# A hybrid decoder block on one core: the two-level FFN products with the weight sums of the second product traced one tile later, the fourth token-side sum traced inside the first tile, and the first tile's operands in other buffers

## The chip, the cores and the metric

The kernel is one program on one core of a Trainium2 chip. The metric is the device time of one execution in microseconds (us); smaller is better. The engines are PE (TensorE), DVE (VectorE), ACT (ScalarE), POOL (GpSimd) and SP (SyncE, which here only issues DMAs). Times inside the program count from the first instruction of the profiled execution (the span's start).

## The reference, cut to what matters

One layer of a hybrid block over 1024 tokens and 16 meta tokens, model width 1024: three mixers (window attention, forgetting attention, a gated recurrence), merged and added to the residual, and then the FFN, which is where the change lies:

```
u = rms_norm(h, norm_ffn[l])
gate_ff, up_ff = jnp.split(u @ w_ffn_in[l], 2, axis=-1)
h = h + (jax.nn.silu(gate_ff) * up_ff) @ w_ffn_out[l]
...
return rms_norm(h, norm_final)[:, N_META:]
```

`w_ffn_in` is 1024 x 5632 (2816 gate columns and 2816 up columns), `w_ffn_out` is 2816 x 1024.

## The kernel before

**Precision.** Every matrix operand is split into a high part (an ACT copy, line 118) and a low part (a DVE subtraction of the high part from the value, line 119); a product is three matmuls (high x high, high x low, low x high, line 150). So each operand costs one ACT and one DVE instruction before PE may use it.

**The FFN's first product.** The 2816 features are 22 tiles of 128. Feature tiles `j` (0 to 10) and `j + 11` form a pair. The tokens are two halves of 512, kept as feature-major operands `u2[0]` and `u2[1]`, each in quarters (`b11`, `b21` of the first half of the tokens, `b12`, `b22` of the second). Pair 0 is computed plainly by `swiglu_plain(0)` and `swiglu_plain(11)`. All other tiles use a two-by-two Strassen-like scheme in `swiglu(f, ...)`: seven `product` calls of 12 matmuls each instead of eight. Its token-side operands are `b11`, `b21`, `b22` and four sums `t1` to `t4`, which `combine()` makes once for all tiles: DVE subtractions and additions on 128x1024 pieces (in rotating buffers `fo`, four of them), and then a split of each. Its weight-side operands are `a11`, `a12` (halves of the gate weights), `a21`, `a22` (halves of the up weights) and sums of these that POOL makes (`a21 - a11`, `s2 = a22 - a21`, `a11 + s2`, `a12 - s2`). `operand` splits a weight-side half into one buffer: the tag `wh` (two buffers), `wl` (two) or `ar` (three).

The seven products of one `swiglu`, in PE's order, by the names of the profile: `a11*b11` into `mm_s` (operand in `wh`), `a12*b21` into `sc_s` (in `wl`), `s2*t2` on top of `mm_s` (in `ar`), `(a11+s2)*t1` into `tr_s` (in `ar`), `a21*t3` on top of `mm_s` (in `ar`), `(a12-s2)*b22` on top of `tr_s` (in `wh`), and `a22*t4` on top of `mm_s` (in `wl`). Before the third product may add to `mm_s`, ACT copies it out (line 952); that copy is named `c`. Results go to the tag `a` (six buffers, two for each `swiglu`).

**Sums for the FFN's second product.** The second product, `product2` at the end, is a two-by-two scheme of the same kind over all 11 pairs. Its sums are made pair by pair in the loop over `j`: `combine_w(j)` loads two tiles of `w_ffn_out` into `fo` buffers, makes four POOL sums and writes four pieces to DRAM (`bsp`); `combine_a(j, a11, a21, a12, a22)` takes the pair's four results, makes four POOL sums and writes six pieces (`asp`); `spill(0, j, ...)` writes the seventh.

**What sets the order.** The Tile framework places every instruction in its engine's queue at compile time. The place in the program is a priority: of the instructions that its planner holds to be ready, the earliest in the program goes first, so a later instruction can stand ahead of an earlier one that isn't ready. Buffers of a tag are handed on when all readers of the old content are done. At run time each queue is in order.

Of the kernel before, what the change touches and what calls it, by code (L numbers as in the profile page):

```python
# [51 lines left out]
def hybrid_block(ctx, tc, h_in, w_in, w_v0, w_v1, w_bd, par, rows, gains, relt, onehot,  # L52
# [4 lines left out]
    def dma(dst, src):  # L57
        nc.sync.dma_start(f32(dst) if dst.dtype == F32R else dst, f32(src) if src.dtype == F32R else src)
# [8 lines left out]
    wp = ctx.enter_context(tc.tile_pool(name="wstream", bufs=2, side="left"))  # L67
# [11 lines left out]
    def nm(s):  # L79
        uid[0] += 1  # L80
        return f"{s}_{uid[0]}"
# [61 lines left out]
    def mm3(ps, terms, first=True):  # L143

        n = 3 * len(terms)
        cost = ps.shape[-1] / 2.4 + 3
        i = 0
        for ah, al, bh, bl in terms:
            for a, b in ((ah, bh), (ah, bl), (al, bh)):
                pe.matmul(ps, a, b, start=first and i == 0, stop=i == n - 1, skip_group_check=not first)  # L150
                i += 1
            yield 3 * cost

    def run(gen):
        for _ in gen:
            pass
# [38 lines left out]
    def halves(x):  # L195
        return x[:, :512], x[:, 512:]
# [80 lines left out]
    with tc.tile_pool(name="r0", bufs=1, side="right", reuse_waits="tile") as r0:  # L277
# [68 lines left out]
        bb = r0.tile([P, 8, 383], F32, name="bb")  # L346
# [128 lines left out]
    with ExitStack() as ctx2:  # L475
# [247 lines left out]
        ready = set()  # L723
# [32 lines left out]
    mp = ctx4.enter_context(tc.tile_pool(name="m4", bufs=16, side="left", reuse_waits="tile"))  # L756
# [7 lines left out]
    def pair_tile(pl, **kw):  # L764

        return [pl.tile([P, D], F32R, tag="m4", name=nm("pt"), **kw).rearrange("p (k t) -> p k t", k=2)
                for a in range(2)]
# [63 lines left out]
    with tc.tile_pool(name="r4", bufs=1, side="right", reuse_waits="tile") as r4:  # L831
        woh = r4.tile([P, KT, D], F32R, name="woh")
        wol = r4.tile([P, KT, D], F32R, name="wol")
        with tc.tile_pool(name="r4a", bufs=1, side="right", reuse_waits="tile") as r4a:
# [8 lines left out]
            for m in range(8):  # L843
                f, raw = ahead
# [50 lines left out]
    NJ = NF // 2  # L895
# [3 lines left out]
    def sub(eng, o, a, b):  # L899
        eng.tensor_tensor(o, a, b, ALU.subtract)  # L900

    def add(eng, o, a, b):
        eng.tensor_tensor(o, a, b, ALU.add)

    with tc.tile_pool(name="r5", bufs=1, side="right", reuse_waits="tile") as r5:
        def t5(tag, bufs, n=512):
            return r5.tile([P, n], F32, tag=tag, bufs=bufs, name=nm(tag))

        def product(ps, a, b, first=True):

            run(mm3(ps, [(a[:, 0, k * P:(k + 1) * P], a[:, 1, k * P:(k + 1) * P],
                          b[k // 2][0][:, k % 2], b[k // 2][1][:, k % 2]) for k in range(4)], first))

        def operand(pl, tag, bufs, src):
            t = pl.tile([P, 2, 512], F32R, tag=tag, bufs=bufs, name=nm(tag))
            split(t[:, 0], t[:, 1], src)
            return t

        def swiglu_plain(f):
            w = [load_w(w_fi[f + NF * i], D) for i in range(2)]  # L920
            at_ = []
            for c in range(2):
                pg, pv = (mm_bank(f"_{x}{f}") for x in "gu")
                for ps, (wh, wl) in zip((pg, pv), w):
                    run(mm3(ps, [(wh[:, k * P:(k + 1) * P], wl[:, k * P:(k + 1) * P],
                                  u2[c][k // 2][0][:, k % 2], u2[c][k // 2][1][:, k % 2]) for k in range(KT)]))
                sg = t5("a", 6)
                act.activation(sg, pg, AF.Sigmoid)
                dve.tensor_tensor(sg, pg, sg, ALU.mult)
                dve.tensor_tensor(sg, pv, sg, ALU.mult)  # L930
                at_.append(sg)
            return at_

        def fetch_fi(f, i):
            w = []
            for s in range(2):
                pl = r5 if i % 2 else wp
                raw = pl.tile([P, D], F32, tag="wr", bufs=2, name=nm("wr"))
                dma(raw, w_fi[f + NF * s])
                w.append(halves(raw))  # L940
            return w

        def swiglu(f, w, bb):

            (a11, a12), (a21, a22) = w
            b11, b21, b22, t1, t2, t3, t4 = bb
            p1, p2, p5 = mm_bank(f"_s{f}"), sc_bank(f"_s{f}"), tr_bank(f"_s{f}")
            g0, g1, u1 = (t5("c", 6) for _ in range(3))
            s0, s1 = (t5("a", 6) for _ in range(2))
            s2 = t5("s2", 2)  # L950
            product(p1, operand(wp, "wh", 2, a11), b11)
            act.activation(g0, p1, AF.Copy)  # L952
            product(p2, operand(wp, "wl", 2, a12), b21)
            add(dve, g0, p2, g0)
            act.activation(s0, g0, AF.Sigmoid)
            dve.tensor_tensor(s0, g0, s0, ALU.mult)
            sub(pool, a21, a11, a21)
            sub(pool, s2, a22, a21)
            product(p1, operand(r5, "ar", 3, s2), t2, False)
            act.activation(g1, p1, AF.Copy)  # L960
            add(pool, a11, s2, a11)
            product(p5, operand(r5, "ar", 3, a11), t1)
            act.activation(u1, p5, AF.Copy)
            product(p1, operand(r5, "ar", 3, a21), t3, False)
            add(dve, u1, p1, u1)
            sub(pool, a12, a12, s2)
            product(p5, operand(wp, "wh", 2, a12), b22, False)
            add(dve, g1, p5, g1)
            act.activation(s1, g1, AF.Sigmoid)
            dve.tensor_tensor(s1, g1, s1, ALU.mult)  # L970
            dve.tensor_tensor(s1, u1, s1, ALU.mult)
            product(p1, operand(wp, "wl", 2, a22), t4, False)
            dve.tensor_tensor(s0, p1, s0, ALU.mult)
            return [s0, s1]

        def combine():

            b11, b21 = u2[0][:2], u2[0][2:]
            b12, b22 = u2[1][:2], u2[1][2:]
            t3 = [pair_tile(r5, bufs=4) for _ in range(2)]  # L980
            t2, t1 = ([pair_tile(mp) for _ in range(2)] for _ in range(2))
            temp = lambda: t5("fo", 4, D).rearrange("p (k t) -> p k t", k=2)
            v2 = []
            for i in range(2):
                v3 = temp()
                v2.append(temp())
                for v, x, y in zip((v3, v2[i]), b22[i], b12[i]):
                    sub(dve, v, f32(x), f32(y))
                add(dve, v3, v3, v2[i])
                for x, y in zip((v3, v2[i]), b11[i]):  # L990
                    add(dve, v2[i], x, f32(y))
                split(*t2[i], v2[i])
                split(*t3[i], v3)
            t4 = [pair_tile(mp) for _ in range(2)]
            for t, b in ((t1, b22), (t4, b21)):
                for i in range(2):
                    v = temp()
                    sub(dve, v, f32(b[i][0]), v2[i])
                    add(dve, v, v, f32(b[i][1]))
                    split(*t[i], v)  # L1000
            return b11, b21, b22, t1, t2, t3, t4

        def spill(i, j, x):
            dma(asp[i][j], x)

        def combine_w(j):

            raws = []
            for i in range(2):
                raw = t5("fo", 4, D)  # L1010
                dma(raw, w_fo[(j + NJ * i) * P:(j + NJ * i + 1) * P])
                raws += halves(raw)
            b11, b12, b21, b22 = raws
            t2 = zp.tile([P, 512], F32, tag="z", bufs=2, name=nm("t2"))
            sub(pool, b12, b22, b12)
            add(pool, t2, b12, b11)
            sub(pool, b11, b22, t2)
            sub(pool, b21, b21, t2)
            for i, x in ((2, t2), (3, b11), (4, b12), (6, b21)):
                dma(bsp[i][j], x)  # L1020

        def combine_a(j, a11, a21, a12, a22):

            s2 = zp.tile([P, 512], F32, tag="z", bufs=2, name=nm("t2"))
            spill(1, j, a12)
            spill(6, j, a22)
            sub(pool, a21, a11, a21)
            sub(pool, s2, a22, a21)
            add(pool, a11, s2, a11)
            sub(pool, a12, a12, s2)  # L1030
            for i, x in ((2, s2), (3, a11), (4, a21), (5, a12)):
                spill(i, j, x)


        for j in range(NJ):
            if j == 0:
                first, second = swiglu_plain(0), swiglu_plain(NJ)
                bb = combine()
                spill(0, j, first[0])
            else:  # L1040
                first = swiglu(j, fetch_fi(j, 0), bb)
                spill(0, j, first[0])
                second = swiglu(j + NJ, fetch_fi(j + NJ, 1), bb)
            combine_w(j)
            combine_a(j, *first, *second)
    ctx4.close()


# [173 lines left out]
```

## Time and profile before

| | us |
|---|---|
| median of 3 runs (1662.05 to 1663.47) | 1662.32 |
| profiled execution, its own time | 1662.29 |
| its span, first to last instruction | 1660.5 |
| PE busy | 1630.2 (98%) |
| DVE busy | 999.4 (60%) |
| ACT busy | 760.7 (46%) |
| POOL busy | 433.1 (26%) |

The span is cut by the work of PE almost everywhere; what lies around the span is 1.8 us. The FFN's plain pair runs from 1008 to 1053 us of the span, the ten pairs of the scheme from there to 1444, and the second product to 1654.

### The profile page before, as it was taken

How to read it: one execution, taken by the hardware profiler on the slowest of the kernel's cores; microseconds unless marked ns; L12 is line 12 of the kernel's file. 1: busy time of each engine (PE TensorE's matmuls, PEld its weight loads, DVE VectorE, ACT ScalarE, POOL GpSimd, SP SyncE). 2: the span in 40 equal slices, each digit the busy share in tenths (PEclk: the TensorE clock that was granted, in tenths of full speed). 3: DMA queues.
4: the chain of work that ended last, by engine and by line, in shares of the span. 5: the costliest groups of instructions: out<-in, count | busy, mean ns of one | idle time of the engine just before them, and what ended most of it. 6: DMA issues, size and time to landing. Idle time of an engine off the chain costs nothing.

```text
span 1660.5 us, 22597 instructions
## 1 busy us (share of the span) xinstructions
PE 1630.2 (98%) x8159; PEld 1375.1 (83%) x8159; DVE 999.4 (60%) x1799; ACT 760.7 (46%) x1397; POOL 433.1 (26%) x341
## 2 busy tenths in 40 slices
PE   7999999999999999999999999899999999999998
PEld 6898978888888888888887888688888888888886
DVE  6565556555566666641348437977666676567544
ACT  6456466555555555542336434333333333345342
POOL 2111001001122221110225001776666566300000
PEclk9999999999999999999999999899999999999999
DMA  7132352223324142339737221464444443598642
GB/s 255 63 108 93 122 153 79 88 89 121 108 76 129 59 122 79 107 114 320 244 127 235 102 77 70 158 222 169 165 147 146 146 161 131 197 356 278 195 128 101
DMA packets 110879, 242.47 MB, mean 146 GB/s; under 512 B 11944, under 2 KB 23544, under 8 KB 110512
## 3 DMA queue, kind: packets, MB, share of 16 engines
q1 hardware_dynamic: 110768, 241.04, 42.7%
q8 instruction: 64, 1.05, 0.3%
q14 instruction: 47, 0.39, 0.1%
HBM read 163.45 MB, written 72.21 MB: 142 GB/s over the span
## 4 chain that ended last, share of the span: by engine, by line
PE 87%; DVE 4%; issue 4%; ACT 2%; POOL 1%; DMA 1%; SPq 0%; DVEq 0%; POOLq 0%; ACTq 0%
PE mm_w L150 26%; PE mm_s L150 13%; PE tr_s L150 7%; PE mm_br L150 6%; PE mm_wo L150 5%; PE mm_x L1086 4%; PE tr_y L1086 4%; PE sc_y L1086 4%; PE ob L547 3%; PE sc_s L150 3%; PE tr L558 3%; PE mm_v L150 2%; PE ob_x L1086 1%; PE mm_g L150 1%; PE mm_u L150 1%
## 5 line engine op out<-in xcount | busy, mean ns | idle before, releaser
L150 PE MATMUL mm_w<-uh,wh 128*128 128x512 f32 (+2 forms) x744 | 292.6, 393 | 0.0
L150 PE MATMUL mm_w<-uh,wl 128*128 128x512 f32 (+2 forms) x744 | 280.5, 377 | 0.0
L150 PE MATMUL mm_w<-ul,wh 128*128 128x512 f32 (+2 forms) x744 | 279.9, 376 | 0.0
L150 PEld LDWEIGHTS mm_w<-uh,wl 128*128 128x128 f32 x744 | 140.0, 188 | 25.7
L150 PEld LDWEIGHTS mm_w<-uh,wh 128*128 128x128 f32 x744 | 140.4, 189 | 12.7
L150 PEld LDWEIGHTS mm_w<-ul,wh 128*128 128x128 f32 x744 | 140.7, 189 | 11.7
L119 DVE TENSOR_TENSOR ab<-raw,ab 128x1024 fp32r<-128x1024 f32 x77 | 93.0, 1224 | 71.6 <-ACT ab L118 69.6
L118 ACT ACTIVATE ab<-raw 128x1024 fp32r<-128x1024 f32 x77 | 80.9, 1059 | 94.7 <-PE ob_x L1086 23.4
L150 PE MATMUL mm_s<-pt,ar 128*128 128x512 f32 x480 | 117.4, 394 | 3.7 <-ACT c L952 3.7
L118 ACT ACTIVATE wh<-wr 128x1024 fp32r<-128x1024 f32 (+1 forms) x85 | 72.7, 856 | 103.2 <-PE mm_w L150 50.6
L150 PE MATMUL mm_br<-o,wh 128*128 128x512 f32 x384 | 118.3, 389 | 0.0
L119 DVE TENSOR_TENSOR pl<-tr,ph 128x384 fp32r<-128x384 f32 (+2 forms) x160 | 87.4, 555 | 47.0 <-ACT ph L118 43.1
L150 PEld LDWEIGHTS mm_s<-pt,ar 128*128 128x128 f32 x480 | 91.5, 191 | 23.6 <-ACT c L952 4.5
L118 ACT ACTIVATE ph<-tr 128x384 fp32r<-128x384 f32 (+2 forms) x160 | 76.8, 485 | 53.6 <-PE tr L558 51.5
L119 DVE TENSOR_TENSOR wl<-wr,wh 128x1024 fp32r<-128x1024 f32 x45 | 55.6, 1235 | 72.2 <-ACT wh L118 71.9
L648 POOL TENSOR_SCALAR s<-s,sm 128x144 f32<-128x144 f32 (+3 forms) x64 | 48.6, 761 | 172.1 <-DVE sm L647 144.2
L150 PEld LDWEIGHTS mm_br<-o,wh 128*128 128x128 f32 x384 | 72.1, 188 | 14.9
L558 PE MATMUL tr<-ident,s 128*128 128x128 f32 x480 | 79.6, 274 | 1.2 <-POOL s L596 0.6
L150 PE MATMUL mm_wo<-woh,hl 128*128 128x512 f32 x256 | 79.1, 390 | 0.0
L150 PE MATMUL mm_br<-o,wl 128*128 128x512 f32 x192 | 75.3, 392 | 1.5 <-DVE wl L119 1.4
L558 PEld LDWEIGHTS tr<-ident,s 128*128 128x128 f32 x480 | 59.1, 140 | 18.3 <-DVE pl L119 3.4
L1086 PE MATMUL mm_x<-ab 128*128 128x512 f32 x297 | 72.7, 389 | 0.0
(252 smaller groups left out, 3687.9 us busy)
## 6 DMA issues: line engine op xcount, KB each, us to landing
wr<-w_in_dram SPq DMA_DIRECT2D x45, 512.0 KB, 3.7
wr<-w_fi_dram SPq DMA_DIRECT2D x44, 512.0 KB, 3.8
raw<-asp SPq DMA_DIRECT2D x77, 256.0 KB, 3.2
asp<-a SPq DMA_DIRECT2D x66, 256.0 KB, 2.5
gz<-z SPq DMA_DIRECT2D x48, 256.0 KB, 2.1
o<-osp SPq DMA_DIRECT2D x24, 512.0 KB, 6.1
sg<-gz SPq DMA_DIRECT2D x48, 256.0 KB, 3.2
fo<-w_fo_dram SPq DMA_DIRECT2D x22, 512.0 KB, 5.1
```

What stands on the lines that cost most here:

```text
L118: act.activation(hi, src, AF.Copy)
L119: i = dve.tensor_tensor(lo, src, f32(hi), ALU.subtract)
L150: pe.matmul(ps, a, b, start=first and i == 0, stop=i == n - 1, skip_group_check=not first)
L547: pe.matmul(ob[:, q0:q0 + b - a], vt[:, c], x[:, a:b], start=count == 0, stop=count == n_mm - 1, skip_group_check=True)
L558: pe.transpose(tb[:, col:col + P], src, ident)
L648: pool.tensor_scalar(s[:, :nk], s[:, :nk], den, 1.0, ALU.mult, ALU.mult)
L1086: pe.matmul(banks[x], a[:, 0, q], b[:, 1], start=first and j == 0 and c == 0, stop=j == NJ - 1 and c % 3 == 2, skip_group_check=True)
```

## The change

`swiglu` takes two optional arguments: operands that are already split (`ready`) and a function that is called before its last product (`fourth`). `combine` no longer makes `t4`; it returns a function that does, and the first `swiglu` calls it. The split of the first tile's `a11` and `a12` is traced ahead of `combine`, into two of the three `ar` buffers (before: `wh` and `wl`). In the loop, `combine_w(j)` and `combine_a(j)` are traced behind `swiglu(j + 1)`, the gate-side half of the next pair, and ahead of `swiglu(j + 12)`. The count of instructions of each kind stays as it was.

```
-        def swiglu(f, w, bb):
+        def swiglu(f, w, bb, ready=None, fourth=lambda: None):
...
-            product(p1, operand(wp, "wh", 2, a11), b11)
+            o1, o2 = ready or (operand(wp, "wh", 2, a11), operand(wp, "wl", 2, a12))
+            product(p1, o1, b11)
             act.activation(g0, p1, AF.Copy)
-            product(p2, operand(wp, "wl", 2, a12), b21)
+            product(p2, o2, b21)
...
             dve.tensor_tensor(s1, u1, s1, ALU.mult)
+            fourth()
             product(p1, operand(wp, "wl", 2, a22), t4, False)
...
-            t4 = [pair_tile(mp) for _ in range(2)]
-            for t, b in ((t1, b22), (t4, b21)):
+            def last_sums(t, b):
                 for i in range(2):
                     v = temp()
                     sub(dve, v, f32(b[i][0]), v2[i])
                     add(dve, v, v, f32(b[i][1]))
                     split(*t[i], v)
-            return b11, b21, b22, t1, t2, t3, t4
+
+            last_sums(t1, b22)
+            t4 = []
+
+            def fourth():
+                t4.extend(pair_tile(mp) for _ in range(2))
+                last_sums(t4, b21)
+            return (b11, b21, b22, t1, t2, t3, t4), fourth
...
+        first, second = swiglu_plain(0), swiglu_plain(NJ)
+        w = fetch_fi(1, 0)
+        ready = [operand(r5, "ar", 3, x) for x in w[0]]
+        bb, fourth = combine()
         for j in range(NJ):
-            if j == 0:
-                first, second = swiglu_plain(0), swiglu_plain(NJ)
-                bb = combine()
-                spill(0, j, first[0])
-            else:
-                first = swiglu(j, fetch_fi(j, 0), bb)
-                spill(0, j, first[0])
-                second = swiglu(j + NJ, fetch_fi(j + NJ, 1), bb)
+            spill(0, j, first[0])
+            pair = first + second
+            if j + 1 < NJ:
+                if j == 0:
+                    first = swiglu(1, w, bb, ready, fourth)
+                else:
+                    first = swiglu(j + 1, fetch_fi(j + 1, 0), bb)
             combine_w(j)
-            combine_a(j, *first, *second)
+            combine_a(j, *pair)
+            if j + 1 < NJ:
+                second = swiglu(j + 1 + NJ, fetch_fi(j + 1 + NJ, 1), bb)
```

## Rows read from the trace of the kernel before

**Rows 1.** The page: busy us of each engine, share of the span, instructions.
```profile
PE 1630.2 (98%) x8159; PEld 1375.1 (83%) x8159; DVE 999.4 (60%) x1799; ACT 760.7 (46%) x1397; POOL 433.1 (26%) x341
```

**Rows 2.** Waits of PE from 1040 us on: total us, times, longest.
```profile
PE mm_s L150 <- ACT c L952: 3.7, 1, 3.7
PE sc_s L150 <- DVE wl L119: 2.0, 1, 2.0
PE mm_s L150 <- DVE wh L119: 0.9, 1, 0.9
```

**Rows 3.** Timeline of PE: start, us, operation, count [idle before, releaser].
```profile
1047.15 0.39 PE L150 MATMUL mm_g<-pt,wl 128*128 128x512 f32 x1
...
1052.82 0.61 PE L150 MATMUL mm_s<-pt,wh 128*128 128x512 f32 x2
...
1066.68 4.96 PE L150 MATMUL mm_s<-pt,ar 128*128 128x512 f32 x12 [3.75 <-ACT c L952]
1071.48 2.88 PE L150 MATMUL tr_s<-pt,ar 128*128 128x512 f32 x12
1074.20 2.88 PE L150 MATMUL mm_s<-pt,ar 128*128 128x512 f32 x12
```

**Rows 4.** Busy time by window; PEclk is the granted clock's share.
```profile
1062.94:1071.48 8.54, 4.79 (x13) 3.80 (x13) 6.72 (x6) 2.37 (x5) 7.83 (x6) 0.53 0.54 209
```

**Rows 5.** Timeline of DVE around the first tile of the scheme.
```profile
1054.20 3.44 DVE L119 TENSOR_TENSOR pt<-fo,pt 128x1024 fp32r<-128x1024 f32 x2
1057.57 1.75 DVE L119 TENSOR_TENSOR wl<-wr,wl 128x512 fp32r<-128x512 f32 x1
...
1067.18 1.77 DVE L119 TENSOR_TENSOR wl<-wr,wl 128x512 fp32r<-128x512 f32 x1
```

**Rows 6.** Timeline of ACT: the copy of line 952 and what stood ahead.
```profile
1065.52 0.63 ACT L118 ACTIVATE wh<-wr 128x512 fp32r<-128x512 f32 x1 [7.25 <-POOL wr L900]
1066.05 0.58 ACT L952 ACTIVATE c<-mm_s 128x512 f32<-128x512 f32 x1
```

**Rows 7.** Timeline of POOL in the same stretch.
```profile
1046.47 4.38 POOL L900 TENSOR_TENSOR s<-wr 128x512 f32<-128x512 f32 x2
...
1063.78 1.71 POOL L900 TENSOR_TENSOR wr<-wr,s 128x512 f32<-128x512 f32 x1
```

**Rows 8.** Timeline of SP's queue: a fetch, the first and a later pair's spills.
```profile
1028.76 0.33 SPq L58 DMA_DIRECT2D wr<-w_fi_dram  x1
...
1068.42 2.00 SPq L58 DMA_DIRECT2D asp<-a  x2
...
1148.77 0.32 SPq L58 DMA_DIRECT2D asp<-a  x1
```

**Rows 9.** The page: DMA issues, KB each, median us to landing.
```profile
wr<-w_fi_dram SPq DMA_DIRECT2D x44, 512.0 KB, 3.8
...
asp<-a SPq DMA_DIRECT2D x66, 256.0 KB, 2.5
```

**Rows 10.** Windows: length, busy of PE, PEld, DVE, ACT, POOL, clock, DMA share.
```profile
1013.87:1068.95 55.08, 48.41 (x202) 38.80 (x201) 52.66 (x49) 20.15 (x29) 28.49 (x14) 0.92 0.28 96
1110.00:1148.16 38.16, 38.16 (x170) 31.60 (x169) 27.34 (x29) 14.49 (x25) 25.41 (x18) 1.00 0.45 159
```

**Rows 11.** Groups on DVE from 1110 to 1400 us: count, busy, mean ns.
```profile
L956 DVE TENSOR_TENSOR a<-c,a 128x512 f32<-128x512 f32 x16 | 19.8, 1234 | 0.0
...
L903 DVE TENSOR_TENSOR c<-tr_s,c 128x512 f32<-128x512 f32 x15 | 10.4, 692 | 17.3 <-PE tr_s L150 17.3
```

**Rows 12.** The tile fo from 1010 to 1110 us: ns min/median/max.
```profile
L903 DVE TENSOR_TENSOR fo<-fo,pt x8: 1210/1219/2305, 1020.1 to 1051.9; 128x1024 f32<-128x1024 f32 x8
...
L900 POOL TENSOR_TENSOR fo<-fo,fo x4: 1287/1294/2246, 1056.5 to 1099.5; 128x512 f32<-128x512 f32 x4
```

**Rows 13.** Timeline of POOL: the last sum of a pair.
```profile
1147.00 1.74 POOL L900 TENSOR_TENSOR a<-a,t 128x512 f32<-128x512 f32 x1
```

**Rows 14.** Timeline of ACT: first write to a new buffer a.
```profile
1164.89 0.63 ACT L955 ACTIVATE a<-c 128x512 f32<-128x512 f32 x1
```

## The prediction

> **What bounds the kernel now.** I read the page first: PE is busy 98% of the span, and no other engine is above 60% [rows 1]. So only what PE does or waits for can move the end; DVE, ACT and POOL matter where PE waits for them. The second view is therefore PE's list of waits. From the FFN's scheme to the end it has three entries, 3.7 + 2.0 + 0.9 = 6.6 us, once each, all into tiles `mm_s` and `sc_s` [rows 2]. Once each means that the wait isn't the loop's: it lies at one place, the first tile of the scheme.
>
> The third view, PE's timeline, gives the whole loss there. The first product starts at 1052.82, the third ends where the fourth starts, at 1071.48; undisturbed, a product of 12 matmuls takes 1074.20 - 1071.48 = 2.72 us [rows 3]. So three products took 18.66 us where 8.16 would do: 10.50 us are lost. Of these 6.6 are the waits; the other 3.9 are a slower PE: between 1062.94 and 1071.48 the mean granted clock was 0.53 of full [rows 4], that is mostly the lower of its two levels (1.2 of 2.4 GHz), after the engine had stood still for 3.75 us [rows 3]. If the waits go, those 3.9 us go with them.
>
> Why does PE wait? DVE's timeline shows the low parts of the first tile's operands queued behind the sums of `combine`: the two splits of `t4` take 3.44 us from 1054.20, and only then, at 1057.57, comes the `wl` operand of the second product [rows 5]. Before the third product, ACT must copy `mm_s` out; its queue stood 7.25 us at the split of `a12 - s2`, which waited for a POOL sum, and the copy came at 1066.05 [rows 6]. That POOL sum ran only at 1063.78 [rows 7]: it overwrites `a12`, so the split of `a12` on DVE had to be over, and POOL had sums of the second product ahead of it. DVE is the root: from 1013.87 to 1068.95 it was busy 52.66 of 55.08 us [rows 10]. Behind the first tile the loop leaves it 38.16 - 27.34 = 10.8 us of slack in each pair [rows 10].
>
> **The change part by part.** Nothing is added or removed; all is order and place.
>
> *First operands into `ar`.* Before, they shared `wh` with the plain pair, whose gate matrix PE read until 1047.15 + 0.39 [rows 3]. The `ar` buffers are free from the start. The raw weights were issued at 1028.76 [rows 8] and land 3.8 us later [rows 9], at 1032.6; two splits traced ahead of `combine` can then be done some 15 us before 1052.82. Cost: the same two DVE and two ACT instructions, earlier. This removes the waits before the first and second product. It fills the ring `ar`, so that `a11 + s2` must wait for the first product's end at 1055.54 and `a21` for the second's at 1058.26; use is at 1060.98 and 1063.70. ACT 0.63 [rows 6], a DVE split of up to 1.77 [rows 5] and one DVE operation ahead, up to 2.31 [rows 12], make 4.7 us of the 5.44 at hand. Bounds 0 to about 1 us, if two operations stand ahead; I take 0, since one is the usual case.
>
> *The fourth sum later.* Two subtractions, two additions and two splits, at 1.22 us each undisturbed [rows 12], 7.3 us of DVE, now stand behind what the first six products need. `t4` is due at the seventh product, 1052.82 + 6 x 2.72 = 1069.14. This is the tight term. Up to 1068.95 DVE had done all splits and sums for the seven products, with the low part of `a22` last [rows 5], in 52.66 busy us [rows 10]. By 1069.14 it must now also do what came later before, because PE was late: three additions from PSUM at 0.69 and three multiplications at up to 1.23 [rows 11], 5.8 us. That makes 58.5 us in 55.27. So the seventh product is late by between 0 (if POOL gets less in DVE's way) and 3.2 us. I take 1.4, near the middle, as neither row is nearer.
>
> *The copy of line 952.* With `a12` split early, POOL can make `a11 + s2` and `a12 - s2` right behind `s2`, which took until 1046.47 + 4.38 = 1050.85 at the latest [rows 7]; two more at up to 2.25 [rows 12] end by 1055.4, as the first product ends. So ACT has nothing late ahead of the copy. Bounds: nothing, or the wait as it was, 3.75 plus what the clock then lost, (1071.48 - 1066.68) - 2.72 = 2.08 [rows 3], together 5.8. I take nothing and keep 5.8 as a rival.
>
> *Sums of the second product one tile later.* Per pair the moved step has eight POOL sums and 13 DMAs (two loads, eleven writes), moved past the gate half's two fetches on SP and its four sums on POOL. Where POOL and SP aren't late, this costs PE nothing: POOL is busy 25.41 of 38.16 us [rows 10]. What could be late is the buffer `a`: six, of which four hold the old pair and two the new gate half, so that the token half's first write waits for the old pair's spills. In an ordinary pair the last sum runs at 1147.00 [rows 13], its spill is issued at 1148.77 [rows 8] and lands 2.5 us later [rows 9], at 1151.3; the write it holds back comes at 1164.89 [rows 14]. That leaves 13.6 us, and four POOL sums moved ahead take 4 x 1.74 [rows 13] = 7.0. For the first pair, now 10.5 us earlier, less is left: its last spills left by 1070.42 [rows 8], so land by 1072.9, and the write is due at 1071.86 + 6.4 = 1078.2 (6.4 is how far the write at 1164.89 lies behind the start of its half, two products and their copies). 5.3 us are left; with two sums moved ahead 1.8, with four a wait of 1.7. I take 0, with 1.7 as the other end.
>
> **The sum.** 10.5 - 1.4 = 9.1 us off the profiled execution's 1662.29, which is within 0.03 of the median: 1653.2. Everything behind 1071.48 moves forward as one piece, for PE has no wait there [rows 2].
>
> **A rule against it.** The same DVE addition takes 1.21 us at its shortest and 2.31 at its longest, and a POOL sum 1.29 to 2.25 [rows 12], while DVE additions that read PSUM stay at 0.69 on the mean [rows 11]. The Trainium skill, page "SBUF — State Buffer", section "Who interferes with whom", says that DVE and GpSimd share one pair of ports under an exclusive lock, and that whoever comes second blocks fully. The rows agree in that an SBUF operation of DVE grows by about one POOL operation. By that rule at its worst, with a POOL sum ahead of each DVE operation, the time would be some 1662, and by the durations as the rows have them 1653.2; the first rival is this case, worked out from rows.
>
> **The rivals.**
>
> *DVE is held up by POOL throughout.* In the first tile seven splits, three multiplications and six `t4` operations have two SBUF inputs. If each grows by 2.31 - 1.22 = 1.09 us [rows 12], that is 16 x 1.09 = 17.4 us. Some of it is in the 52.66 already, and no row separates how much; if half, the other 8.7 on top of the 3.2 make the seventh product over 10.5 us late, and the gain is gone: 1662. Half as much lateness gives 1657. For it: POOL must do the same sums in less time. Against: POOL was busy only 28.49 of 55.08 us [rows 10], so it can't meet every one. Chance 0.12.
>
> *The planner leaves ACT blocked before line 952 again.* The queue order is set by estimates, and they were wrong here by 7.25 us before [rows 6]. Then 5.8 us stay: 10.5 - 5.8 = 4.7 saved, 1657.6. Against: what ACT waited for loses its reasons. Chance 0.10.
>
> *Nothing is gained.* The planner could order DVE by readiness much as before, with `t4` again ahead; against it, the first two operands are ready long before. About 1662. Chance 0.06.
>
> *Slower: the buffer `a` becomes the wait.* If the old pair's spills come over 13.6 us later than now in every pair, PE stands once per pair in each of ten. Each us beyond 13.6 costs 10; slower than before by 3.3 needs (10.5 + 3.3)/10 = 1.4 beyond, so 15 us late; 2 us beyond gives 1662 - 9 + 20 = 1673. For it: POOL's and SP's queues are now ordered with the sums behind the next gate half. Against: the moved-ahead sums explain 7.0 us, not 15, and POOL has 12.7 us idle in a pair [rows 10]. Chance 0.12.
>
> **How the numbers follow.** The forecast, the wait gone but for up to about 4 us, has 0.60: 1651.5 (nothing late) to 1656. About 0.2% of the time, 3.3 us, is what a measurement can tell from no change. Faster by more: 0.60, the blocked copy's 0.10, and half of the first rival, 0.06: 0.76. Same: the other half and the case without gain: 0.12. Slower: 0.12. The range, 1651.4 to 1660.0, takes in the forecast, the blocked copy and the better part of the first rival, some 0.8.
>
> **What would show it.** Right: PE's waits in `mm_s` and `sc_s` gone or short, the granted clock at full across 1053 to 1072, the first two splits of the tile on DVE before 1050, the fourth product's start near 1061, the end of the FFN's first product near 1435 instead of 1444, no new wait of PE in the loop. Wrong on the tight term: a wait before the seventh product, on DVE's `wl` or `pt`. Wrong on the whole: one wait of the same kind in each pair, with ACT at line 955 waiting for a DMA of `a`, or ACT standing again before line 952.

## The result, and the profile after

The change made the kernel slower: 1668.89 us median (1668.19 to 1673.15) against 1662.18 of the kernel before, a ratio of 1.0044 with a 95% interval of 1.0031 to 1.0057. Forecast were 1653.2 us, and the likeliest rival on the slower side isn't what happened either. The page of the kernel after, its span and the line of the engines: PE does the same matmuls in nearly the same busy time as in [rows 1], and the span has grown by 1667.1 - 1660.5 = 6.6 us.

```profile
span 1667.1 us, 22606 instructions
...
PE 1631.8 (98%) x8159; PEld 1376.0 (83%) x8159; DVE 990.7 (59%) x1799; ACT 759.9 (46%) x1397; POOL 433.8 (26%) x341
```

PE's waits from 1045 us on (us in total, times, longest):

```profile
PE mm_s L150 <- ACT c L954: 6.0, 1, 6.0
PE mm_s L150 <- DVE c L903: 4.3, 2, 3.4
PE mm_s L150 <- DVE a L930: 0.7, 1, 0.7
```

Beside [rows 2]: the waits for `wh` and `wl` are gone, but the one for ACT's copy (line 952 before, 954 now) has grown from 3.7 to 6.0, and there is a new one, for DVE's `c`, at two places. PE's timeline gives the places:

```profile
1053.75 2.98 PE L150 MATMUL mm_s<-pt,ar 128*128 128x512 f32 x12 [0.67 <-DVE a L930]
1056.57 2.88 PE L150 MATMUL sc_s<-pt,ar 128*128 128x512 f32 x12
1065.49 4.98 PE L150 MATMUL mm_s<-pt,ar 128*128 128x512 f32 x12 [6.04 <-ACT c L954]
1070.31 2.91 PE L150 MATMUL tr_s<-pt,ar 128*128 128x512 f32 x12
...
1094.82 2.88 PE L150 MATMUL tr_s<-pt,wh 128*128 128x512 f32 x12
1101.14 5.49 PE L150 MATMUL mm_s<-pt,wl 128*128 128x512 f32 x12 [3.45 <-DVE c L903]
...
1109.58 2.88 PE L150 MATMUL sc_s<-pt,wl 128*128 128x512 f32 x12
...
1120.46 2.88 PE L150 MATMUL tr_s<-pt,wh 128*128 128x512 f32 x12
1124.17 3.02 PE L150 MATMUL mm_s<-pt,wl 128*128 128x512 f32 x12 [0.82 <-DVE c L903]
1127.02 2.88 PE L150 MATMUL mm_s<-pt,wh 128*128 128x512 f32 x12
```

On names: the prediction and the expectations call `swiglu(j + 1)` the gate half and `swiglu(j + 12)` the token half of a pair. In the kernel each of them is a whole feature tile, with its gate and its up columns and all tokens. Below they go by the call: `swiglu(1)` is the first tile of the scheme, `swiglu(12)` the second, `swiglu(2)` the third.

Measured as in the prediction, with 2.72 us for a product: the first three products lose (1070.31 - 1053.75 + 0.67) - 8.16 = 9.1 us, where they lost 10.50 before. Three products from 1094.82 on, the last two of `swiglu(12)` and the first of `swiglu(2)`, lose (1109.58 - 1094.82) - 8.16 = 6.6, and two from 1120.46 on, the last of `swiglu(2)`, lose (1127.02 - 1120.46) - 5.44 = 1.1. That is 16.8 against 10.5, and the scheme's first product began 0.3 us later: 6.6 in all, the whole growth of the span. So the first tile gained next to nothing, and a place that lost nothing before lost 7.7.

**The first tile.** DVE, ACT, POOL and SP's queue in it:

```profile
1037.85 1.22 DVE L903 TENSOR_TENSOR fo<-fo,pt 128x1024 f32<-128x1024 f32 x1
1038.99 0.68 DVE L929 TENSOR_TENSOR a<-mm_g,a 128x512 f32<-128x512 f32 x1
1039.59 1.72 DVE L119 TENSOR_TENSOR pt<-fo,pt 128x1024 fp32r<-128x1024 f32 x1
1048.84 1.93 DVE L119 TENSOR_TENSOR pt<-fo,pt 128x1024 fp32r<-128x1024 f32 x1 [7.52 <-ACT pt L118]
...
1062.13 1.22 DVE L903 TENSOR_TENSOR fo<-fo,pt 128x1024 f32<-128x1024 f32 x1
```

```profile
1047.22 0.63 ACT L118 ACTIVATE ar<-s 128x512 fp32r<-128x512 f32 x1 [8.84 <-POOL s L900]
1047.76 1.04 ACT L118 ACTIVATE pt<-fo 128x1024 fp32r<-128x1024 f32 x1
...
1063.38 1.06 ACT L118 ACTIVATE pt<-fo 128x1024 fp32r<-128x1024 f32 x1 [2.97 <-DVE fo L903]
...
1064.86 0.58 ACT L954 ACTIVATE c<-mm_s 128x512 f32<-128x512 f32 x1
```

```profile
1033.41 6.82 POOL L900 TENSOR_TENSOR a<-a,a 128x512 f32<-128x512 f32 x1 [15.43 <-DVE a L930]
1044.53 1.29 POOL L900 TENSOR_TENSOR wr<-wr,wr 128x512 f32<-128x512 f32 x1 [4.30 <-DMA wr<-w_fi_dram]
1045.90 2.54 POOL L900 TENSOR_TENSOR s<-wr 128x512 f32<-128x512 f32 x2
...
1049.65 2.27 POOL L900 TENSOR_TENSOR wr<-wr,s 128x512 f32<-128x512 f32 x1
```

```profile
1040.26 0.33 SPq L58 DMA_DIRECT2D asp<-a  x1
1040.63 0.43 SPq L58 DMA_DIRECT2D wr<-w_fi_dram  x1
```

Read from the end. PE's third product needs ACT's copy at 1064.86. Ahead of it in ACT's queue stand high parts of `pt`, the last at 1063.38, which waited for DVE's sum of 1062.13: that is `t4`, which was to come later, still ahead of what the third product needs. DVE was so late because it stood 7.52 us, to 1048.84, for a high part of `pt` that was ready to be made but stood behind `ar<-s` in ACT's queue. That split stood 8.84 us for POOL's `s`, which waited for raw weights, whose fetch SP issued only at 1040.63, behind a spill of a POOL sum that took 6.82 us. In the kernel before, ACT stood at `ar<-s` just as long, which [rows 6] doesn't show:

```profile
1037.91 1.06 ACT L118 ACTIVATE pt<-fo 128x1024 fp32r<-128x1024 f32 x1 [0.61 <-DVE fo L903]
1048.66 0.64 ACT L118 ACTIVATE ar<-s 128x512 fp32r<-128x512 f32 x1 [9.69 <-POOL s L900]
```

But there the high part that DVE needed next had been made at 1037.91, ahead of `ar<-s`, and DVE went on with the sums of `t1` and `t4` meanwhile. In the changed kernel DVE splits the first operands into `ar` from 1034.38 to 1035.67; the token sum of that high part ends 1.2 us later (1039.07 against 1037.88), and in ACT's queue `ar<-s` now stands ahead of it.

**The second tile, `swiglu(12)`.** The same engines 35 us later:

```profile
1099.80 0.69 DVE L119 TENSOR_TENSOR ar<-wr,ar 128x512 fp32r<-128x512 f32 x1 [8.18 <-ACT ar L118]
1100.40 0.68 DVE L903 TENSOR_TENSOR c<-mm_s,c 128x512 f32<-128x512 f32 x1
```

```profile
1064.57 4.06 POOL L900 TENSOR_TENSOR fo<-fo,fo 128x512 f32<-128x512 f32 x1 [12.66 <-DVE a L930]
...
1089.33 1.74 POOL L900 TENSOR_TENSOR fo<-fo,fo 128x512 f32<-128x512 f32 x1
...
1097.84 1.26 POOL L903 TENSOR_TENSOR wr<-s,wr 128x512 f32<-128x512 f32 x1
```

```profile
1057.68 4.89 SPq L58 DMA_DIRECT2D fo<-w_fo_dram  x3
...
1080.17 0.99 SPq L58 DMA_DIRECT2D wr<-w_fi_dram  x2
```

PE's seventh product waits for DVE's `c` at 1100.40. It stood behind the low part of the next tile's `a11 + s2`, which waited 8.18 us for its high part, that for POOL's sum at 1097.84, and that behind six sums of the second product (1089.33 to 1097.8). POOL was late from 1064.57 on, after 12.66 us without work. The trace puts these down to DVE's line 930, which ended at 1064.55 behind the token sums. The sum that POOL then began reads `fo`, whose loads were issued from 1057.68 to 1062.2, as DVE's splits of `t1` and `t4` gave the buffers back; a run below shows that this load isn't what set the time. The next weights were fetched at 1080.17, in SP's queue behind the spills of that work.

### The profile page after: what moved, and what is told of

The parts are those of the page before. It is cut to its first block, busy times and chain, and to the rows that moved or that the text cites. A ratio compares the mean times of both kernels' runs of the same rounds, so it can differ in the third digit from the quotient of the medians.

```text
span 1667.1 us, 22606 instructions
## 1 busy us (share of the span) xinstructions
PE 1631.8 (98%) x8159; PEld 1376.0 (83%) x8159; DVE 990.7 (59%) x1799; ACT 759.9 (46%) x1397; POOL 433.8 (26%) x341
## 4 chain that ended last, share of the span: by engine, by line
PE 79%; DVE 7%; issue 5%; POOL 3%; DMA 3%; ACT 3%; SPq 0%; DVEq 0%; POOLq 0%; ACTq 0%
PE mm_w L150 24%; PE mm_s L150 11%; PE tr_s L150 6%; PE mm_br L150 6%; PE mm_wo L150 5%; PE mm_x L1100 4%; PE tr_y L1100 4%; PE sc_y L1100 4%; PE ob L547 3%; PE tr L558 3%; PE sc_s L150 3%; PE mm_v L150 2%; PE ob_x L1100 1%; PE sc L632 1%; PE sc L633 1%
```

## The experiments

Eighteen kernels ran, each timed against the kernel before in the same batch. The last columns are PE's loss over 2.72 us a product, in the profiled execution: in the first three products (from the end of the plain pair's last matmul, 0.1 us more than above), and in all later ones of the FFN's first product (from the fourth product's start to the second product's first matmul, less 137 x 2.72). They tell more than the spans, since the work ahead of the scheme ended anywhere between 1051.7 and 1054.6.

| run | median us | ratio to before (95%) | first three | later |
|---|---|---|---|---|
| before | 1662.18 | 1 | 10.5 | 0 |
| the change | 1668.89 | 1.0044 (1.0031 to 1.0057) | 9.2 | 7.7 |
| loop_only | 1660.35 | 0.9986 (0.9977 to 0.9995) | 8.4 | 0.5 |
| fourth_only | 1671.09 | 1.0049 (1.0037 to 1.0062) | 5.5 | 12.9 |
| ready_only | 1662.64 | 1.0004 (0.9995 to 1.0013) | 9.4 | 2.1 |
| ready_fourth | 1667.74 | 1.0030 (1.0018 to 1.0042) | 1.3 | 15.0 |
| before_early_fetch | 1661.79 | 0.9998 (0.9989 to 1.0007) | 9.8 | 0 |
| full_early_fetch | 1663.27 | 1.0007 (0.9999 to 1.0016) | 2.4 | 9.0 |
| loop_early_fetch | 1659.76 | 0.9987 (0.9978 to 0.9996) | 8.2 | 0.8 |
| ready_loop_early | 1660.35 | 0.9989 (0.9980 to 0.9998) | 1.8 | 8.6 |
| full_w_later | 1668.14 | 1.0037 (1.0024 to 1.0050) | 9.0 | 5.9 |
| full_early_w_later | 1663.55 | 1.0005 (0.9996 to 1.0013) | 1.1 | 8.2 |
| ready_early_w_later | 1660.80 | 0.9993 (0.9985 to 1.0001) | 1.1 | 4.4 |
| fourth_early_w_later | 1659.38 | 0.9982 (0.9974 to 0.9991) | 4.3 | 1.4 |
| full_first_sums_late | 1663.08 | 1.0008 (0.9999 to 1.0016) | 9.4 | 0.8 |
| fourth_first_sums_late | 1661.31 | 0.9997 (0.9988 to 1.0006) | 6.9 | 3.0 |
| full_early_first_sums_late | 1655.67 | 0.9964 (0.9950 to 0.9978) | 1.1 | 2.4 |
| fourth_loop_early_first_sums_late | 1657.74 | 0.9971 (0.9960 to 0.9982) | 3.9 | 1.9 |
| before_first_sums_late | 1660.01 | 0.9984 (0.9975 to 0.9993) | 5.0 | 3.0 |
| ready_loop_early_first_sums_late | 1656.87 | 0.9967 (0.9954 to 0.9979) | 1.1 | 2.8 |

**One part of the change at a time.** Each run takes the lines of one part from the diff (the loop; `fourth`; `ready`) and leaves the rest as before; ready_fourth takes two.

```
loop_only:    combine_w(j); combine_a(j, *pair)      # behind swiglu(j + 1)
fourth_only:  first = swiglu(1, fetch_fi(1, 0), bb, fourth=fourth)
ready_only:   first = swiglu(1, w, bb, ready=ready)
ready_fourth: first = swiglu(1, w, bb, ready=ready, fourth=fourth)
```

loop_only:


> Only the sums of the second product are traced one tile later; t4 and the first operands stay as before. If the new waits of the changed kernel at its seventh product of the second and third halves (6.6 and 1.1 us) come from this part, they are here too and the first tile still loses about 10.5: some 1670, 7 to 8 us slower than before. If they come from the later t4 or the other buffers, this kernel is within 2 us of before.


fourth_only:


> Only the fourth token-side sum is traced inside the first tile. My theory: DVE then has nothing to do while ACT's queue stands at the split of s2, idles some 7 us, and the first tile's loss stays near 10 us: 1662 give or take 2. Rival (the forecast's own step): DVE was simply overfull, so taking 7 us of t4 off its way brings the loss down to 4 or less: 1656.


ready_only:


> Only the first two operands are split early into ar buffers. The waits before the first and second product (1.1 and 2.2 us, with 1.1 of slower clock) go; the copy of line 952 remains late unless ACT's queue changes: 2 to 4 us faster, 1658 to 1660, if the late copy has its own cause; 8 or more faster, if the first two operands were the root of all.


ready_fourth:


> The change without its loop part. If the loop part alone makes the later waits, this kernel has the changed kernel's first tile (9.2 us lost) and nothing behind it: 1661, 1 us faster than before, 7.7 faster than the changed kernel. If the later waits come from the first tile's parts, it is as slow as the changed kernel, 1669.

The loop part gains some 2 us, the operands in `ar` change nothing in the time, and the fourth sum alone costs as much as the whole change. The first theory after the result was that the loop part brings the later waits; with loop_only faster than before, it fell. Neither time expected of fourth_only came (1671.09), nor that of ready_only (1662.64); ready_fourth came near its second case, 1669, but without the changed kernel's first tile.

ready_only has that first tile, with `t4` in `combine` and the loop as before. PE's wait for the copy and DVE's for the high part are those of the change within 0.1 us:

```profile
1065.36 5.05 PE L150 MATMUL mm_s<-pt,ar 128*128 128x512 f32 x12 [6.02 <-ACT c L953]
```

```profile
1048.72 1.94 DVE L119 TENSOR_TENSOR pt<-fo,pt 128x1024 fp32r<-128x1024 f32 x1 [7.56 <-ACT pt L118]
```

So DVE's stand comes with the first operands' new place and doesn't need the fourth sum's. All five kernels with these operands and the late fetch have it (7.5 to 7.8 us); those without these operands wait at most 0.6 us for that high part. With the fourth sum moved alone DVE does run out of work, and stands 5.58 us at the low part of `ar<-s`, but the first three products lose 5.5 us instead of 10.5. ready_fourth shows what else it takes:

```profile
1050.78 1.94 DVE L119 TENSOR_TENSOR pt<-fo,pt 128x1024 fp32r<-128x1024 f32 x1 [7.79 <-ACT pt L118]
...
1068.77 3.51 DVE L900 TENSOR_TENSOR fo<-pt,fo 128x1024 f32<-128x1024 f32 x2 [6.13 <-DMA bsp<-fo]
```

```profile
1074.01 4.42 PE L150 MATMUL tr_s<-pt,ar 128*128 128x512 f32 x10 [9.41 <-DVE ar L119]
```

DVE stands as in the change, but `t4` is behind the copy, and the first three products lose 1.3 us. The fourth then waits 9.41 us for a low part behind `t4`'s sums, which wait for a write-out of `fo`. Where the fourth sum alone loses, DVE and ACT show:

```profile
1062.91 4.02 DVE L900 TENSOR_TENSOR fo<-pt,fo 128x1024 f32<-128x1024 f32 x2 [1.66 <-DMA bsp<-fo]
```

```profile
1069.20 1.06 ACT L118 ACTIVATE pt<-fo 128x1024 fp32r<-128x1024 f32 x1 [7.54 <-DVE fo L903]
...
1072.15 0.57 ACT L960 ACTIVATE c<-mm_s 128x512 f32<-128x512 f32 x1
```

DVE's `t4` sums wait 1.66 us for a write-out, `bsp<-fo`: the first pair's weight sums had taken the `fo` buffers, and `t4` gets them when these sums have left for DRAM. ACT stands 7.54 us at the high part of `t4`, for that wait and DVE's `t4` operations behind it, and makes the copy of line 960 behind it; PE's fifth product waits 4.3 us for that copy. In the changed kernel it is the other way about: the loop part puts the weight sums behind, `t4` has the buffers first, and its sums are ahead of the third product's copy again.

**Raw weights early.** The raw weights of `swiglu(j + 1)` go to the two buffers that are free from the start, those of `swiglu(j + 12)` to the two that wait for the plain pair:

```
-        w = fetch_fi(1, 0)
+        w = fetch_fi(1, 1)
...
-                    first = swiglu(j + 1, fetch_fi(j + 1, 0), bb)
+                    first = swiglu(j + 1, fetch_fi(j + 1, 1), bb)
...
-                second = swiglu(j + 1 + NJ, fetch_fi(j + 1 + NJ, 1), bb)
+                second = swiglu(j + 1 + NJ, fetch_fi(j + 1 + NJ, 0), bb)
```

full_early_fetch, the whole change with it:


> The whole change, but the gate half's weights use the pair of raw buffers that is free at 1010 us and the token half's the other pair, so that the first tile's a21 and a22 need not wait for the fetch at 1040.6. My theory: ACT no longer stands 8.8 us at the split of s2, DVE no longer idles 7.5 us, t4's sums and with them the fo buffers come some 7 us earlier, and both the first tile's loss (9.2) and the later ones (7.7) shrink: 8 to 14 us faster than the changed kernel, 1655 to 1660. Rival: DVE is overfull whatever the fetch does; then no more than 2 us come back.


before_early_fetch, the kernel before with it:


> The kernel before with the raw buffers of the two halves exchanged and nothing else. If the late fetch was behind its 10.5 us too, 4 to 8 us faster, some 1656; if its DVE queue alone was, within 2 us of before.


loop_early_fetch, the loop part with it:


> The loop part alone with the raw buffers exchanged. Additive: 2.2 us of the loop part and what the exchange gives to the kernel before; some 1654. If the loop part's 2 us come from the same wait that the exchange removes, it equals the exchange alone.


ready_loop_early, the whole change but for the fourth sum's move:


> Loop part and early first operands with the raw buffers exchanged, t4 as before. With the fetch early, the first two operands in ar take the waits before products one and two (4.4 us in all with the slower clock): the first tile's loss under 4, some 1653 to 1656. If t4 then fills DVE ahead of the third product's operands, no better than the loop part with the exchange.

In the changed kernel the first three products now lose 2.4 us instead of 9.2, with `t4` still ahead of the copy. ready_fourth kept the stand and lost 1.3. So in a kernel with these operands it takes both: ACT's stand at `ar<-s`, with a token sum's high part behind it, and `t4` ahead of the copy; without either the loss goes. In the kernel before the same edit gains nothing measurable (9.8 us lost): there DVE's own queue was full, as [rows 10] has it. Only that expectation held. loop_early_fetch gained nothing over loop_only, and full_early_fetch and ready_loop_early stayed behind what was expected, since both lose about 9 us later. ready_loop_early does so with `t4` in `combine`, so the later loss isn't bound to the fourth sum's new place. The seventh product of `swiglu(12)` waits on all the same in full_early_fetch:

```profile
1096.64 4.62 PE L150 MATMUL mm_s<-pt,wl 128*128 128x512 f32 x10 [4.89 <-DVE c L903]
```

**The weight sums of every pair behind `swiglu(j + 12)`.** `combine_w(j)` is traced behind the second `swiglu` call of each pass:

```
-            combine_w(j)
             combine_a(j, *pair)
             if j + 1 < NJ:
                 second = swiglu(j + 1 + NJ, fetch_fi(j + 1 + NJ, 1), bb)
+            combine_w(j)
```

full_w_later, the whole change:


> The whole change, but combine_w(j) is traced one half later still, behind the next token half, so that POOL's queue is not headed by a sum that waits for an fo buffer. My theory: fo buffers, held by the later t4 and v2, stop POOL for 12.7 us, and the spills, the fetch behind them in SP's queue and the sums for the third half are late for that; so the 7.7 us lost at the seventh products of the second and third halves go, the first tile's 9.2 stay: 1660 to 1662, 7 to 9 faster than the changed kernel. Rival: the sums themselves are too many for POOL there; then 3 us or less come back.


full_early_w_later, with early raw weights as well:


> Both repairs: raw buffers exchanged and combine_w one half later. If the two causes are independent, some 7 us go at each: first tile 2.4 lost, nothing behind it, 1653 to 1655, 8 us faster than before. If POOL is overfull, the later waits stay and it is 1659 or more.


ready_early_w_later, that without the fourth sum's move:


> Both repairs with t4 made ahead of the first tile as before. If the later t4 is worth what the forecast said once the two waits are gone, this one is 3 to 6 us slower than the kernel with both repairs, 1657 to 1660; if t4's place is indifferent then, within 1 us of it.


fourth_early_w_later, with that move, but without operands in `ar`:


> Both repairs with the later t4, but the first operands in wh and wl as before. If the ar buffers matter, the waits before the first and second product come back, 2 to 4 us slower than the kernel with both repairs; if not, the same within 1 us.

This only moved the wait: in full_w_later the products at the end of `swiglu(12)` lose 1.0 us instead of 6.6, but those at the end of `swiglu(2)` lose 4.1 instead of 1.1, and the second product waits 1.7 for its first operands. The rival came, 0.75 us back instead of 7 to 9, and full_early_w_later lies in its second case, 1659 or more. Against both expectations, that kernel gets faster when either the fourth sum's move (1660.80) or the operands in `ar` (1659.38) are taken out. So the place of the step mattered, but these four don't say why.

**The first pair's weight sums alone, out of the way.** These are the sums of pair 0, the plain one. Their result is needed only in the second product. They are traced with those of pair 3, all else stays:

```
-            combine_w(j)
+            for i in {0: (), 3: (3, 0)}.get(j, (j,)):
+                combine_w(i)
```

full_first_sums_late:


> The changed kernel (1668.9), but the first pair's weight sums (two loads into fo buffers, four POOL sums, four writes) are traced with those of pair 3; nothing else moves, and the values are the same. Theory: the later waits of PE in the changed kernel (6.6 us before the seventh product of the first pair's token half, 1.1 after it) come from this step, whose loads wait for the fo buffers that the late fourth sums hold, and which stands at the head of POOL's queue for 12.7 us. Then these 7 to 8 us go and only the 9.2 us of the first tile stay: 1661 to 1662.5. Rival: the step is only one of several things queued on POOL and SP, and the wait comes back at another place: 1666 or more.


fourth_first_sums_late:


> The kernel before with only the fourth sum moved (1671.1), and the first pair's weight sums traced with those of pair 3. Theory: with that move alone the fourth sum stands behind the write-out of the first pair's weight sums, since both use the four fo buffers, and that is where 8.5 us were lost; without that user the sums find free buffers: 1657 to 1661 (first tile some 5.5 us, a later wait of up to 3). Rival: the order of DVE and ACT is what loses them, and the buffers are only the last to come free: 1667 or more.


full_early_first_sums_late:


> The changed kernel with the raw-weight buffers of the two halves exchanged (1663.3), and the first pair's weight sums traced with those of pair 3. Theory: the first tile loses 2.4 us as it did with the exchange alone, and the 8.9 us lost later (7.3 and 1.6) go: 1654 to 1656.5, what the change was predicted to give. Rival: the later losses stay for 5 us or more: 1660 or more.


fourth_loop_early_first_sums_late:


> The change without the first operands in ar, with the raw-weight buffers of the two halves exchanged, and the first pair's weight sums traced with those of pair 3. Theory: as the run before, but with the waits for the first operands: first tile some 4 to 8 us, nothing later: 1657 to 1661. Rival: later losses of 4 us or more stay, 1662 or more.

PE's waits in the changed kernel with that edit, and POOL in it:

```profile
PE mm_s L150 <- ACT c L953: 6.0, 1, 6.0
PE mm_s L150 <- DVE a L930: 0.7, 1, 0.7
PE mm_s L150 <- DVE c L903: 0.5, 1, 0.5
```

```profile
1065.79 4.00 POOL L900 TENSOR_TENSOR t<-a,a 128x512 f32<-128x512 f32 x1 [12.71 <-DVE a L930]
...
1094.32 1.29 POOL L903 TENSOR_TENSOR wr<-s,wr 128x512 f32<-128x512 f32 x1
```

The first tile's wait is the same 6.0 us, the later ones are down from 4.3 to 0.5, and their loss from 7.7 to 0.8 us. In one point the expectation was wrong: POOL's 12.7 us of idle time stayed (to 1065.79), so it isn't the first sum's wait that costs. What went is work: the next tile's `a11 + s2` comes at 1094.32, 3.5 us before 1097.84, since one set of sums less stands ahead. The DMAs of that step left SP's queue with it (the next weights were fetched at 1077.83 instead of 1080.17), and the run doesn't separate the two. The time, 1663.08, is 0.6 above the range expected; this execution's scheme began 1.1 us later than that of the changed kernel. With the fourth sum alone the later loss falls from 12.9 to 3.0, and the time is 0.3 above its range; the other two are inside theirs. With early raw weights and this edit the whole change takes 1655.67 us, PE's waits in it are

```profile
PE mm_s L150 <- DVE c L903: 1.7, 2, 1.0
PE mm_s L150 <- ACT c L953: 0.8, 1, 0.8
```

and it is the fastest kernel of the study: 6.2 us below the 1661.89 of the kernel before in its batch.

**Two controls.** The same edit on the kernel before, and the best kernel with the fourth sum back in `combine`:

before_first_sums_late:


> The kernel before with only the first pair's weight sums traced with those of pair 3. Theory: a control. Before has no wait of PE behind the first tile, so the step costs it nothing to lose, and the gain that the changed kernel has from it (5.8 us) is not to be had here: within 2 us of before, 1660 to 1664. Rival: the step holds up the first tile in before as well, so that its delay is a gain of its own: 1659 or less, and then the effect isn't one of the buffers held by the fourth sum.


ready_loop_early_first_sums_late:


> The kernel of the best run so far (1655.7: the whole change, raw-weight buffers exchanged, first pair's weight sums with those of pair 3) with the fourth sum back in combine. Theory: with the raw weights early and the fo buffers free, the late fourth sum saves the 6 to 8 us of DVE work ahead of the fourth product that this kernel still has in its way (with the weight sums at their place it was 1660.4): 1658 to 1661. Rival: the fourth sum's place gains nothing even then, and the two delays alone make the gain: 1654 to 1656.5.

In the kernel before the edit gains 2.75 us by itself, more than the 2 us expected of a control: the first pair's weight sums were in the way there too (the first three products lose 5.0 us instead of 10.5, and 3.0 come back later). If gains add, which no run tests, about 3 of the 5.8 us that it gave the changed kernel, and 7 of the 9.8 that it gave the fourth sum alone, are owed to what these kernels do differently. The second control speaks against the theory: its 1656.87 lies between the two ranges, without the fourth sum's move the best kernel loses 3.9 us of PE's time in place of 3.5, and the ratios, 0.9967 and 0.9964, can't be told apart. Its wait has only moved to the fourth product:

```profile
PE tr_s L150 <- DVE ar L119: 2.4, 1, 2.4
```

## Why the prediction was wrong

**Right: where the kernel lost.** One place, 10.5 us in the first three products, and the low clock as a consequence of the wait. Kernels that take the waits away run these products with 1.1 us lost and at nearly full clock. The first two operands came in time; PE's 0.7 us before them were for a PSUM bank that DVE's line 930 read late. In the changed kernel the clock follows the wait at both places; windows (length, busy of PE, PEld, DVE, ACT, POOL, granted clock, DMA share, GB/s):

```profile
1061.60:1070.31 8.71, 4.82 (x12) 3.81 (x13) 8.71 (x11) 3.73 (x6) 5.74 (x3) 0.61 0.54 181
1098.00:1109.58 11.58, 8.44 (x24) 6.67 (x25) 5.02 (x6) 2.82 (x5) 6.54 (x5) 0.71 0.66 235
```

Of its two levels, 1.2 and 2.4 GHz, PE thus has the lower one for the most part of the first stretch. A wait of 3.45 us became a loss of 6.6 this way.

**Wrong: "The copy of line 952", taken as nothing.** The reason given held: POOL had all four sums of the tile done by 1051.9, ahead of the predicted 1055.4. But it was not the only thing that ACT could stand at. ACT's queue also holds the high parts of the token sums; each waits for a DVE sum, and `t1` and `t4` came late. The rival of the blocked copy named the right place, at 5.8 us; measured were 6.2 until the third product begins and 2.1 of slow clock. ACT standing again before that copy was also one of the signs given for being wrong. It was called unlikely because what ACT waited for had lost its reasons; the wait came from another instruction in the same queue.

**Wrong: the cost of "First operands into `ar`".** It was given as the same instructions, earlier, and taken as nothing. But in ACT's queue a token sum's high part fell behind `ar<-s`, and DVE stood idle for 7.52 us. ready_only has this without the other two parts, and its first three products lose 9.4. The prediction had read ACT's stand of 7.25 us before the copy, but not the one of 9.69 us at `ar<-s`, where the high part then ended up.

**Wrong: "The fourth sum later", 0 to 3.2 us.** The term counted DVE's busy time: 58.5 us of work in 55.27. DVE was not overfull, as it stood idle for 7.52 us. And moving `t4` in the program didn't move it behind the third product's needs in the queues: with the loop part, its sums came where they come with `t4` in `combine` (the last at 1062.13, in ready_only at 1061.42). Without the loop part it did move, and the first three products lost 5.5 and 1.3 us, as the step had meant; but then it waited for `fo`, and 12.9 and 15.0 us were lost behind. In full_early_fetch, without ACT's stand, the first three products lose 2.4 with `t4` where it was.

**Wrong: "Everything behind 1071.48 moves forward as one piece".** 7.7 us were lost there. The step on the second product's sums asked of the buffer `a` only, and that rival didn't come: no run has a wait of PE for a write-out of it in the loop. It did not ask how POOL's work for the second product stands to its work for the next tile, once both are late, nor of `fo`, the buffers that these sums and `t4` share. That the first pair's weight sums cost it is shown: 7.7 down to 0.8 with them out of the way. Whether by POOL's time or by SP's queue isn't; a wait of DVE for a write-out of `fo` shows only in kernels without the loop part. The loop part by itself did no harm, as predicted at 0, and gained 2 us.

The losses add up: the predicted gain of 9.1 us was lost to the first block (9.2 of 10.5 stayed), and 7.7 us of new loss came on top. Both removed, with the raw weights early, the time is 1655.67, inside the range that was given for the change as it was. That is another kernel and no support for the forecast; and then `t4` may as well stay in `combine`.

Open stays why full_early_first_sums_late still waits 1.7 us for DVE's `c`, and what part of the 12.7 us that POOL stands idle could be had. The change without the fourth sum's move alone, with the late fetch, wasn't run, so what that move costs inside the change isn't measured. Deeper `fo` buffering wasn't tried.

## What to carry to other kernels

When instructions are traced earlier, find the instruction in each in-order queue that stands still, and ask what ready work now falls behind it, on that engine and on those that wait for it: here two short splits put one high part behind a stand of 9 us. A later place in the program isn't a later place in a queue; look there whether the step moved. For each buffer tag that the moved step uses, list every other user and ask who now holds it when; a sum of busy times sees none of this. If several steps collide at one place, try removing one that isn't due yet: here the first pair's weight sums, not needed for more than 350 us, were worth more (2.75 us) than the edit that was planned.

## What the runs showed of the hardware

A POOL sum that takes 1.29 us (1044.53) took 6.82 at 1033.41, and 6.74 in the kernel before. Through all 6.82 us DVE ran without a gap, its operations at their usual 1.22; it was POOL that got no turn. It ended 1.24 us after the DVE operation of 1038.99 began, the first in that stretch with an operand in PSUM, and the DVE operation after that, with both inputs in SBUF, took 1.72 in place of 1.22. The same happened at 1064.57: 4.06 us, while DVE split operands in its usual 0.68 and 1.22, ending 1.22 us after DVE's next read of PSUM:

```profile
1066.81 0.68 DVE L119 TENSOR_TENSOR ar<-wr,ar 128x512 fp32r<-128x512 f32 x1
1067.41 0.68 DVE L903 TENSOR_TENSOR c<-sc_s,c 128x512 f32<-128x512 f32 x1
```

The Trainium skill, page "SBUF — State Buffer", section "Who interferes with whom", has DVE operations with two SBUF inputs and GpSimd contend for one port pair, held for a whole instruction. The trace agrees, and adds that back-to-back DVE operations can keep POOL out for several instructions. The prediction's rival by that rule had DVE held up by POOL; in the stretch that mattered, at 1033.41, it was POOL that stood, and through it SP's queue, the weights' fetch, ACT and then DVE itself.
